# Taking the mean squares of attention results by pairs of tiles beside the last head

## The chip, the core and the metric

The kernel runs on one core of one Trainium2 chip. The metric is the device time of one execution in microseconds (us). Three runs of the kernel before took 2566.53 to 2570.46 us; their median is 2568.71 us.

## The reference, cut to what matters

One post-norm layer is computed for 2048 prompt frames and 8 streams of 16 new frames, 2176 tokens in all. A combined projection feeds a gated convolution and a differential attention of 4 heads with 128 values each. The attention result of each token and head is divided by its root mean square before the output projection:

```python
def rms_norm(x, g):
    xf = x.astype(jnp.float32)
    ms = jnp.square(xf).mean(-1, keepdims=True)
    return (xf * lax.rsqrt(ms + LN_EPS) * g.astype(jnp.float32)).astype(x.dtype)
...
    attn_o = rms_norm(attn_o, subln_g) * (1.0 - lambda_init)
    mixed = jnp.concatenate([y_conv, attn_o.reshape(B, S, ATTN_DIM)], axis=-1)
    x1 = layer_norm(ALPHA * x + jnp.einsum('bse,ed->bsd', mixed, w_out), ln1_g, ln1_b)
```

The mean runs over the 128 values of one head. After this come a feed-forward part (1024 to 4096 to 1024, squared ReLU) and a second layer norm.

## The kernel before, in words

The tokens are 17 tiles of 128 (NT = 17; tile 16 holds the new frames). Everything on TensorE (PE) is fp32 or made of split high and low parts (`mm3`, lines 71 to 73: three matmuls per product). The program has three stages.

1. The input projection (to about 500 us in the trace) writes q, k, v and the gated convolution result to DRAM.
2. The attention loop (lines 874 to 894) walks over head h = 0 to 3 and, in each head, over pairs of query tiles jp = 7 down to 0 (tiles 2jp and 2jp+1). Each pair has a front (scores, maxima, exponentials) and a back (scaling, transposes, values). `merge` interleaves by cost the front of one pair with the back of the pair before and with a share of the fill. The fill is 17 x 9 steps that multiply the convolution result by its half of w_out (`conv_half`, L841 to L867) and write the sum with the residual to `mixd` in DRAM. `finish_av` (L561 to L564) copies the result of one pair out of PSUM (tile `af`) and writes it to `attn` in DRAM with SP's queue. The tile of new frames is done inside each head beside jp = 6, 5, 4 (`decode_steps`).
3. The output projection of the attention half, then the feed-forward part. For each tile t in `ORDER` (11, 16, 10, 15, 9, 14, 8, 13, 7, 12, 6, 5, 4, 3, 2, 1, 0) three helpers are called:
   - `mix_rms(t)` (L933 to L946) loads the tile's four heads from `attn` (L936, SP's queue, tile `at`), squares them on ScalarE (ACT, L938, tile `sq`), takes the means over the partitions with four one-column matmuls against a column of 1/128 (`meand`, L941; each fp32 matmul is two instructions), copies the 128 x 4 result (L943, VectorE, DVE) and forms the inverse root in `rstd_of` (L896 to L909: a square root on ACT, L899, and a Newton step of five small DVE instructions).
   - `mix_prep(t, at, rms)` (L948 to L963) loads the sum so far from `mixd` (L953, tile `z`), builds four diagonal matrices from the roots (L957, tile `dg`), spreads them with matmuls (L958), multiplies `at` by them (L960) and splits the product (cast to high part on ACT, L64, low part on DVE, L67).
   - `mix_out(t, z, m)` (L981 to L994) makes the 24 matmuls of the projection, adds `z` and, for five tiles, a layer norm; `turn` (L494) transposes those five for the feed-forward part.

Three tiles go through `mix_rms` and two through `mix_prep` in the last `merge` (L966), beside the back of the last pair; then `mix_rms` runs three tiles ahead of `mix_out` and `mix_prep` two.

The tile framework orders the instructions of each engine with a timeline of its own: among instructions that are ready it takes the one that stands first in the program. So loads and weight preparation (L134 to L137, L536) are found earlier in the trace than in the program. Each engine then runs its list in order. Buffers matter as well: tiles with the tag `z` of the pool `mp` have three buffers, which the convolution part, `w_out` loads and two of three tiles of `mix_prep` share; `at` and `sq` share four; the PSUM banks `pt` are three.

## Time and profile before

| what | us |
|---|---|
| runs, lowest, median, highest | 2566.53, 2568.71, 2570.46 |
| the profiled execution's own time | 2571.69 |
| its span, first to last instruction | 2569.9 |
| TensorE (PE) busy | 2469.0 |
| VectorE (DVE) busy | 1877.1 |
| ScalarE (ACT) busy | 1291.4 |
| GpSimd (POOL) busy | 914.0 |
| mean granted PE clock | 0.986 of 2.4 GHz |

How to read it: the span is one execution taken by the profiler; the time of an execution is about 1.8 us longer than its span. Busy time is the union of an engine's instructions. Instructions overlap on PE, and their ends are modelled, so that two matmuls with starts 0.23 us apart have durations of 0.39 us each. "[0.97 <-DVE ml L67]" behind an instruction means that its engine stood 0.97 us before it, and that the instruction on line 67 that writes tile `ml` on DVE ended the wait. Times in a timeline count from the span's start.

### The profile page before, as it was taken

To read this page: it belongs to the slowest core of one execution; us is meant where nothing else is said; L and a number is where in the kernel's file an instruction comes from. 1 tells how busy PE (TensorE), PEld (TensorE's weight loads), DVE (VectorE), ACT (ScalarE), POOL (GpSimd) and SP (SyncE) were. 2 spreads that over 40 slices of the span, in tenths; PEclk is the share of its full clock that TensorE was granted. 3 is DMA by queue.
4 is the path that set the end of the run, shared out by engine and by line. 5 is a ranking of instruction groups with operands and counts; after the bars stand their busy time and mean duration, and the time that the engine had idled before them with its cause. 6 is when DMAs were issued, how large, how long until landed. Compare 5 with 4: busy or idle time off the path is not lost. (4 is left out here: it accounts for less than half of the span.)

```text
span 2569.9 us, 38835 instructions
## 1 busy us (share of the span) xinstructions
PE 2469.0 (96%) x13420; PEld 2243.4 (87%) x13420; DVE 1877.1 (73%) x3103; ACT 1291.4 (50%) x2676; POOL 914.0 (36%) x778
## 2 busy tenths in 40 slices
PE   8999999979999999999998999999998999999998
PEld 7999999968787878779997999999997888888886
DVE  7798677767767776786887888898877535444578
ACT  5444445436757666434677566756553322223231
POOL 5565564547465645231232322322223102115000
PEclk9999999999999999999998999999999999999999
DMA  7437326345535343545678577766667655446444
GB/s 250 156 106 233 127 84 191 104 128 181 166 103 157 118 130 107 193 160 172 197 255 291 190 243 244 274 212 209 216 222 267 213 163 185 148 143 221 153 151 148
DMA packets 273317, 463.24 MB, mean 180 GB/s; under 512 B 32320, under 2 KB 178832, under 8 KB 273120
## 3 DMA queue, kind: packets, MB, share of 16 engines
q1 hardware_dynamic: 260160, 431.58, 51.9%
q10 hardware_dynamic: 11088, 24.12, 2.4%
q0 software_dynamic: 1872, 5.07, 0.6%
q8 instruction: 105, 1.72, 0.3%
q14 instruction: 92, 0.75, 0.1%
HBM read 316.98 MB, written 143.69 MB: 179 GB/s over the span
## 5 line engine op out<-in xcount | busy, mean ns | idle before, releaser
L71 PE MATMUL y<-vh,hrh 128*128 128x512 f32 x832 | 323.1, 393 | 5.6 <-ACT vh L64 5.6
L72 PE MATMUL y<-vl,hrh 128*128 128x512 f32 x832 | 323.9, 389 | 1.5 <-DVE vl L67 1.5
L73 PE MATMUL y<-vh,hrl 128*128 128x512 f32 x832 | 323.5, 389 | 0.0
L64 ACT CAST hrh<-hraw 128x1024 fp32r<-128x1024 f32 x112 | 118.1, 1056 | 344.7 <-PE y L72 328.8
L67 DVE TENSOR_TENSOR hrl<-hraw,hrh 128x1024 fp32r<-128x1024 f32 x112 | 146.0, 1304 | 171.6 <-ACT hrh L64 171.3
L686 ACT ACTIVATE p<-s,nm 128x512 f32<-128x512 f32 (+3 forms) x320 | 199.2, 633 | 98.3 <-DVE nm L684 88.5
L684 DVE TENSOR_REDUCE nm<-s 128x1 f32<-128x512 f32 (+3 forms) x320 | 184.5, 601 | 43.9 <-PE s L679 41.9
L71 PEld LDWEIGHTS y<-vh,hrh 128*128 128x128 f32 x832 | 157.8, 190 | 39.4 <-ACT vh L64 6.5
L72 PEld LDWEIGHTS y<-vl,hrh 128*128 128x128 f32 x832 | 156.3, 188 | 34.6 <-DVE vl L67 2.0
L73 PEld LDWEIGHTS y<-vh,hrl 128*128 128x128 f32 x832 | 156.3, 188 | 32.4
L713 POOL TENSOR_SCALAR p<-p,cf 128x512 f32<-128x512 f32 (+3 forms) x160 | 123.9, 793 | 149.7 <-DVE cf L706 124.0
L134 POOL TENSOR_TENSOR wS<-raw 128x512 f32<-128x512 f32 x78 | 113.6, 1457 | 166.2 <-DVE wS1l L67 100.4
L678 PE MATMUL s<-kt,aq 128*128 128x512 f32 (+3 forms) x344 | 136.5, 405 | 18.5 <-DMA kt<-k_sc 10.7
L762 PE MATMUL pa<-a,vt 128*128 128x256 f32 (+1 forms) x576 | 140.3, 371 | 0.4 <-ACT a L741 0.4
L71 PE MATMUL pf<-x11h,w11h 128*128 128x384 f32 (+1 forms) x324 | 108.7, 336 | 15.9 <-ACT x11h L64 14.5
L679 PE MATMUL s<-kt,ql 128*128 128x512 f32 (+3 forms) x344 | 123.2, 366 | 0.3 <-DMA ql<-q_sc 0.3
L762 PEld LDWEIGHTS pa<-a,vt 128*128 128x128 f32 x576 | 104.2, 191 | 14.5 <-ACT a L741 1.2
L1233 POOL TENSOR_TENSOR t<-wq,t 128x512 f32<-128x512 f32 x32 | 51.9, 1636 | 173.1 <-DMA wq<-w_ff 172.8
L71 PE MATMUL pf<-x22h,wS4h 128*128 128x384 f32 (+1 forms) x324 | 107.2, 331 | 3.9 <-DVE c L182 3.8
L72 PE MATMUL pf<-x11l,w11h 128*128 128x384 f32 (+1 forms) x324 | 108.4, 335 | 1.1 <-DVE x11l L67 1.1
L71 PE MATMUL pf<-x21h,w12h 128*128 128x384 f32 (+1 forms) x324 | 105.8, 327 | 3.2 <-ACT u L174 3.2
L73 PE MATMUL pf<-x11h,w11l 128*128 128x384 f32 (+1 forms) x324 | 107.8, 333 | 0.0
(644 smaller groups left out, 7830.2 us busy)
## 6 DMA issues: line engine op xcount, KB each, us to landing
raw<-w_ff SPq DMA_DIRECT2D x96, 512.0 KB, 4.0
hraw<-hf SPq DMA_DIRECT2D x96, 512.0 KB, 4.1
wq<-w_ff SPq DMA_DIRECT2D x144, 256.0 KB, 3.8
raw<-w_in SPq DMA_DIRECT2D x70, 512.0 KB, 4.3
hf<-h SPq DMA_DIRECT2D x32, 768.0 KB, 3.8
wr<-w_ff SPq DMA_DIRECT2D x32, 512.0 KB, 4.3
xs<-x1d SPq DMA_DIRECT2D x24, 512.0 KB, 5.6
hf<-h SPq DMA_DIRECT2D x32, 384.0 KB, 3.2
```

Of the source, the lines that this page charges most:

```text
L64: nc.scalar.copy(hi, src)
L67: return lo_eng.tensor_sub(lo, src, hi)
L71: nc.tensor.matmul(ps, lh, rh, start=start, stop=False, skip_group_check=more)
L72: nc.tensor.matmul(ps, lh, rl, start=False, stop=False, skip_group_check=more)
L73: nc.tensor.matmul(ps, ll, rh, start=False, stop=stop, skip_group_check=more)
L134: nc.gpsimd.tensor_add(S["S1"], a21, a22)
L678: nc.tensor.matmul(ss[c][:, pos:pos + m], aq[:, c, qsl], kt[:, c], start=True, stop=False)
L679: nc.tensor.matmul(ss[c][:, pos:pos + m], ql[:, c, qsl], kt[:, c], start=False, stop=True)
L684: nc.vector.tensor_reduce(nm[:, qb, ci, c:c + 1], s[:, :kn], axis=AX.X, op=ALU.max, negate=True)
L686: nc.scalar.activation(pt[:, :kn], s[:, :kn], AF.Exp, bias=nm[:, qb, ci, c:c + 1], accum_out=sm[:, qb, ci, c:c + 1])
L713: nc.gpsimd.tensor_scalar(p1[:, :kn], p1[:, :kn], X["cf"][:, qb, ci, 1:2], 1.0, op0=ALU.mult, op1=ALU.mult)
L762: nc.tensor.matmul(o, vt[:, kb % 4, :], a[:, i], start=first, stop=end)
```

## The change

The squares of all tiles are taken for pairs of tiles. For tiles 2 to 16 these steps (`squares`) are put into the back of the next pairs of the last head (h = 3), a quarter of the way in: each loads two tiles of `attn` at once, squares them with one ACT instruction, makes the one-column matmuls of both and copies the means into a table `msq`. Both tiles of a step, the loaded one and the squared one, are `z` buffers of the pool `mp`. Tiles 2 and 3 are taken in the back of the last pair; tile 16 by itself in the back of pair 3. The inverse roots of tiles 2 to 16 are then formed by one call of `rstd_of` on 128 x 60 in the middle of that last back, followed by `mix_prep` of the first two tiles of `ORDER`. Tiles 0 and 1 are squared behind the last `merge`, and their roots are a second call. `mix_rms(t)` per tile is gone; `mix_prep(t)` loads `at` itself, so that each tile of `attn` is read twice. The scratch tiles of `rstd_of` are slices of one tile of the probability pool.

```diff
+        msq = mp_.tile([P, NT, H], F32, name="msq", bufs=1)
+        rms = mp_.tile([P, NT, H], F32, name="rms", bufs=1)
+
+        def squares(t, n):
+
+            def put():
+                at = mp_.tile([P, 4, 2 * P], F32, name="z", bufs=3)[:, :, :n * P]
+                nc.sync.dma_start(at, attn[:, :, t * P:(t + n) * P].rearrange("h p t -> p h t"))
+                sq = mp_.tile([P, 4, 2 * P], F32, name="z", bufs=3)[:, :, :n * P]
+                nc.scalar.activation(sq, at, AF.Square)
+                ps = ps_t.tile([P, 512], F32, name="pt")
+                for i in range(n):
+                    for h in range(H):
+                        k = i * H + h
+                        nc.tensor.matmul(ps[:, k:k + 1], sq[:, h, i * P:(i + 1) * P], meand, start=True, stop=True)
+                nc.vector.tensor_copy(msq[:, t:t + n].rearrange("p n h -> p (n h)"), ps[:, :n * H])
+            return put
...
             pend = back
+            if h == H - 1 and jp < 7:
+                pend.insert(len(pend) // 4, (0.3, squares(2 * jp + 2, 2)))
+            if h == H - 1 and jp == 3:
+                pend.insert(len(pend) // 2, (0.2, squares(NT - 1, 1)))
...
-        def mix_rms(t):
-            s = slice(t * P, (t + 1) * P)
+        class Slices:
+
+
+            def __init__(self, pool):
+                self.home, self.used = pool.tile([P, 512], F32, name="rm", tag="p"), 0
+
+            def tile(self, shape, dtype, name):
+                self.used += shape[1]
+                return self.home[:, self.used - shape[1]:self.used]
+
+        def mix_rms(a, n):
+
+            flat = lambda x: x[:, a:a + n].rearrange("p n h -> p (n h)")
+            rstd_of(Slices(pp), flat(rms), flat(msq), [P, n * H], "rm")
+
+        def mix_prep(t):
             at = mp_.tile([P, 4, P], F32, name="at", bufs=4)
-            nc.sync.dma_start(at, attn[:, :, s].rearrange("h p t -> p h t"))
-            sq = mp_.tile([P, 4, P], F32, name="sq", tag="at", bufs=4)
-            nc.scalar.activation(sq, at, AF.Square)
-            mp = ps_t.tile([P, 512], F32, name="pt")
-            for h in range(H):
-                nc.tensor.matmul(mp[:, h:h + 1], sq[:, h, :], meand, start=True, stop=True)
-            ms = mp_.tile([P, H], F32, name="ms")
-            nc.vector.tensor_copy(ms, mp[:, :H])
-            rms = mp_.tile([P, H], F32, name="rms")
-            rstd_of(mp_, rms, ms, [P, H], "rm")
-            return t, at, rms
-
-        def mix_prep(t, at, rms):
+            nc.sync.dma_start(at, attn[:, :, t * P:(t + 1) * P].rearrange("h p t -> p h t"))
...
-                nc.vector.tensor_scalar(dg, ident, rms[:, h:h + 1], None, op0=ALU.mult)
+                nc.vector.tensor_scalar(dg, ident, rms[:, t, h:h + 1], None, op0=ALU.mult)
...
-        q_rms, q_prep = [], []
-        merge(pend, fill, [(0.2, lambda t=t: q_rms.append(mix_rms(t))) for t in ORDER[:AHEAD + 1]]
-              + [(0.9, lambda: q_prep.append(mix_prep(*q_rms.pop(0))))] * AHEAD)
+        q_prep = []
+        def mix_first(t):
+            return 0.9, lambda: q_prep.append(mix_prep(t))
+
+        mid = len(pend) // 2
+        pend[mid:mid] = [(0.2, lambda: mix_rms(2, NT - 2))] + [mix_first(t) for t in ORDER[:AHEAD]]
+        merge(pend, fill)
+        squares(0, 2)()
+        mix_rms(0, 2)
...
-            if i + AHEAD + 1 < NT:
-                q_rms.append(mix_rms(ORDER[i + AHEAD + 1]))
-            if q_rms:
-                q_prep.append(mix_prep(*q_rms.pop(0)))
+            if i + AHEAD < NT:
+                q_prep.append(mix_prep(ORDER[i + AHEAD]))
```

## Rows read from the trace of the kernel before

**Rows 1.** The page, first section: engine, busy us, share of the span, instructions.

```profile
PE 2469.0 (96%) x13420; PEld 2243.4 (87%) x13420; DVE 1877.1 (73%) x3103; ACT 1291.4 (50%) x2676; POOL 914.0 (36%) x778
```

**Rows 2.** Windows: stretch; busy PE, PEld, DVE, ACT, POOL (instructions); PE clock, DMA share, GB/s.

```profile
1000.00:1053.00 53.00, 49.32 (x286) 41.87 (x285) 37.65 (x115) 31.29 (x87) 26.15 (x34) 1.00 0.48 148
1053.00:1198.00 145.00, 136.57 (x719) 116.79 (x719) 114.37 (x318) 47.36 (x90) 30.18 (x20) 0.95 0.47 163
1075.00:1090.00 15.00, 13.03 (x61) 11.00 (x61) 11.68 (x44) 4.77 (x10) 2.40 (x1) 0.77 0.41 140
1110.00:1125.00 15.00, 12.82 (x75) 10.81 (x76) 13.48 (x38) 4.03 (x9) 5.31 (x4) 1.00 0.60 211
1145.00:1160.00 15.00, 13.11 (x64) 11.18 (x63) 11.56 (x35) 5.28 (x12) 4.34 (x3) 0.77 0.69 227
```

**Rows 3.** Timeline of PE, 1060 to 1150 us: start, us, instruction, [idle before <-releaser].

```profile
1067.65 0.50 PE L73 MATMUL s<-woh,ml 128*128 128x512 f32 x1 [0.97 <-DVE ml L67]
...
1077.03 0.79 PE L71 MATMUL s<-woh,mh 128*128 128x512 f32 x1 [1.97 <-ACT mh L64]
...
1110.46 1.13 PE L958 MATMUL pt<-dg,onesd 128*128 128x128 f32 x8 [1.65 <-DVE x22l L67]
...
1115.70 0.71 PE L958 MATMUL pt<-dg,onesd 128*128 128x128 f32 x4 [1.29 <-DVE dg L957]
...
1147.15 1.18 PE L941 MATMUL pt<-cols,sq 128*128 128x1 f32 x6 [1.89 <-ACT sq L938]
```

**Rows 4.** Tile sq: its matmuls; durations in ns, minimum, median, maximum.

```profile
L941 PE MATMUL pt<-cols,sq x136: 164/250/353, 1041.2 to 1171.6; 128*128 128x1 f32 x136
```

**Rows 5.** Timeline of PE from the last pairs' values to the first projection matmul.

```profile
1041.19 1.84 PE L941 MATMUL pt<-cols,sq 128*128 128x1 f32 x16
...
1044.83 1.68 PE L762 MATMUL pa<-a,vt 128*128 128x256 f32 x8
...
1047.03 0.40 PE L73 MATMUL pt<-wch,ml 128*128 128x512 f32 x1
1048.78 1.05 PE L941 MATMUL pt<-cols,sq 128*128 128x1 f32 x8 [1.35 <-ACT sq L938]
...
1050.05 1.06 PE L958 MATMUL pt<-dg,onesd 128*128 128x128 f32 x8
...
1052.74 0.50 PE L71 MATMUL s<-woh,mh 128*128 128x512 f32 x1
```

**Rows 6.** Timeline of ACT, 1040 to 1050 us.

```profile
1041.83 1.28 ACT L899 ACT_TABLE_LOAD   x1
...
1048.09 0.63 ACT L938 ACTIVATE sq<-at 128x512 f32<-128x512 f32 x1 [4.48 <-DMA at<-attn]
1048.63 0.35 ACT L563 COPY af<-pa 128x256 f32<-128x256 f32 x1
```

**Rows 7.** Tile rms: diagonals and one of the small steps; ns, minimum, median, maximum.

```profile
L957 DVE TENSOR_SCALAR dg<-ident,rms x68: 255/281/746, 1044.3 to 1174.9; 128x128 f32<-128x128 f32 x68
L900 DVE RECIPROCAL rms<-rmsd x17: 158/172/179, 1043.5 to 1172.7; 128x4 f32<-128x4 f32 x17
```

**Rows 8.** Timeline of DVE ahead of PE's stop at 1077.03 us.

```profile
1075.52 0.15 DVE L943 COPY ms<-pt 128x4 f32<-128x4 f32 x1
1075.59 0.74 DVE L960 SCALAR_TENSOR_TENSOR at<-at,cols,pt 128x512 f32<-128x512 f32 x1
```

**Rows 9.** Source line L564, 860 to 1060 us: writes of attention results, 17 of them.

```profile
DMA to landing us min/median/max: 1.7/2.5/5.3
```

**Rows 10.** Source line L936: loads of one tile of attention results (256 KB), 17 of them.

```profile
DMA to landing us min/median/max: 2.8/3.7/11.1
```

**Rows 11.** Source line L826: loads of 512 KB of w_out, four of them.

```profile
DMA to landing us min/median/max: 4.3/4.4/4.5
```

**Rows 12.** Source line L1094: Squares of 1024 columns on ACT, in ns.

```profile
L1094 ACT ACTIVATE sq<-xs,mean x12: 1139/1152/1157, 1198.2 to 1583.4; 128x1024 f32<-128x1024 f32 x12
```

**Rows 13.** Lines, ACT, 1000 to 1200 us: the casts; busy us, mean ns, idle before, releasers.

```profile
L64 ACT CAST mh<-at 128x512 fp32r<-128x512 f32 x17 | 10.5, 619 | 22.4 <-DVE at L960 14.3 <-PE s L72 5.8 <-DVE dg L957 2.3
```

## The prediction

> **What bounds the kernel now.** I read the page's first section before anything else: the matrix engine PE is busy 96% of the span [rows 1], so only two kinds of change can move the end: one in the work that PE does, or one in the time that PE stands or runs slowly. The table of windows then shows the two stretches that the change touches. From 1000 to 1053 us, the end of the last head's attention, PE works 49.32 of 53 us at full clock. From 1053 to 1198 us, which is the output projection and the first products after it, PE works 136.57 of 145 us, so it stands 8.4 us, and its clock is below one: 0.77 in each of two stretches of 15 us [rows 2]. The clock has two levels, 2.4 and 1.2 GHz, so a mean of 0.77 loses 0.23 x 15 = 3.45 us, 6.9 us for both. VectorE (DVE) works 114.37 of the same 145 us, far more than ScalarE (ACT): it is the busiest helper there [rows 2]. PE's timeline names the stops: five of them, of 0.97, 1.97, 1.65, 1.29 and 1.89 us, make 7.8 of the 8.4 us, and what ended them is DVE or ACT work each time [rows 3]. The two low clocks stand behind the stops of 1.97 and 1.89 us; behind 1.65 and 1.29 us the clock stayed at 1.00 [rows 2, 3].
>
> **PE's work is moved, not removed.** The mean squares are 136 one-column matmuls before [rows 4] and stay 136. Sixteen of them in a row take 1.84 us [rows 5], so 17 tiles hold 17 x 8 x 0.115 = 15.6 us. Three tiles' worth stands before 1053 us already [rows 5]; fifteen will (tiles 2 to 16). So about 12 tiles, 11 us, move forward from one stretch where PE is the limit to another: by itself zero. What they can fill in the last head is its idle time, 53 - 49.32 = 3.7 us [rows 2], less the stop of 1.35 us [rows 5] that lies at the change-over below: 2.3 us, of which I take 1.5 (bounds 0 and 2.3).
>
> **New waits in the last head.** Each pair loads its results again by SP's queue, squares them on ACT and needs a "z" buffer for each of the two. ACT serves in order, and a Square put ahead of its data holds what stands behind it: before, one held ACT 4.48 us and a finished result (af) stood behind it [rows 6], and one of the three groups of mean squares in this stretch stopped PE, by 1.35 us [rows 5]. Eight groups move into stretches with exponentials on ACT. At one stop in three this is 8 x 1.35 / 3 = 3.6 us; with other attention work beside them it is zero. I take 0.5, near zero, because ACT's 4.48 us of waiting became only 1.35 us of PE. The second reading of the results adds 17 x 0.26 = 4.5 MB to 148 GB/s x 53 us = 7.8 MB at a DMA share of 0.48 [rows 2]; that is hidden while the queues are half empty, and its price, if not, is a longer landing, in the bounds of the change-over. The three buffers are shared with the loads of x for the convolution part, which run late by a pair's stay; those are needed four matmul groups later, so I price them at nothing; without that cover they would add to the 3.6 us. Together: -1.0 us (bounds -2.3 and +3.6).
>
> **The projection stretch gets freer.** Each tile loses a load wait, a Square of 0.63 us [rows 6], a square root and six small DVE instructions, of which the reciprocal of four columns takes 0.17 us [rows 7]; 15 tiles x 6 x 0.17 = 15 us of DVE's 114, replaced by two rounds. The stop of 1.89 us waited for a Square itself: it goes, with the clock behind it, 5.3 us. The stop of 1.97 us was PE waiting for a cast whose input (at, L960) stood in DVE's queue behind a copy of another tile's mean squares (L943) and what came before it [rows 3, 8]: with a shorter queue it probably goes, with its clock, 5.4 us. The stops of 0.97 and 1.29 us are DVE's backlog too; I count half, 1.1 us. The 1.65 us waits for buffers of the transposes and stays. Against that, tiles 0 and 1 are now squared inside this stretch, late, since their second buffer comes free only when an earlier tile's z does: one more stop like the 1.35 us at two chances in three, 0.9 us. Sum -11 us; the bounds are -5.3 (only the stop that names the Square) and -14.7 (all five and the clock).
>
> **The change-over gets a chain.** This is what the change pays with. Before, the first projected tile (11) has its own roots, from data written long before, and PE starts the projection at 1052.74 us, 6.2 us after the values of the last pair but one end (1044.83 + 1.68 = 1046.5) [rows 5]. After, every tile needs the batch of tiles 2 to 16, and tiles 2 and 3 are that same pair. From the end of its values: copy 0.35, write landing 2.5, load of 512 KB 4.4 (as long as the weights of that size; 3.7 is the median of today's half-size load) [rows 6, 9, 10, 11], Square of 1024 columns 1.15 [rows 12], 16 matmuls 1.84 [rows 5], copy, root and five small steps 7 x 0.18 = 1.3 [rows 7], four diagonals 4 x 0.28 = 1.1 [rows 7], the last of the broadcasts 0.3 of 1.06 [rows 5], the product with "at" 0.74 [rows 8], the cast 0.62 [rows 13]; about eleven hand-overs of 0.06 us (a Square's end at 1048.72 to its matmul at 1048.78 [rows 5, 6]) add 0.7. That makes 15 us. PE's work in it: the 4.9 us it had in those 6.2 us, with 1.84 in place of 0.92 for the squares, 5.8 us, and half of the pair before, 0.9. It stands 8.4 us where it stood 1.35: +7.0. A stop of that length I expect to be followed by the low clock, as the shorter ones of 1.97 and 1.89 us were: +3.4. Sum +10.4 us. Bounds: with the shortest landings (1.7 and 2.8) [rows 9, 10], the whole pair before as filling and no low clock, +3.7; with the longest (5.3 and 11.1) it would be about +20. I take the medians: the queues are half empty (a DMA share of 0.48 [rows 2]), and 11.1 is one landing of 17.
>
> The rows price write and load at 2.5 and 4.4 us [rows 9, 11], and I put one after the other. The Trainium skill, "DMA: Bandwidth & Descriptors", section "Two DMAs through the same engine are not ordered", speaks against the change here: a load of what another DMA writes has to wait for that one's completion, even on the same queue. No row here shows an overlap; with one, the sum would be 2.5 us lower. The same page of the Trainium skill ("Anatomy of one DMA") gives some 2 us as the fixed part of a DMA and 436 GB/s for the rest; an estimate from it is 2.3 and 3.2 us, 1.4 us less than the rows, and the sum would be 1.4 us lower by it. The rows decide.
>
> The square root's table load (1.28 us, once [rows 6]) stays one, since no exponential follows the first root: zero, and in the standing time anyway.
>
> **Sum.** -1.0 - 11 + 10.4 = -1.6 us. The profiled execution took 2571.69 us (span 2569.9), 2.98 us over the median of the runs shown, 2568.71. Against its own time the sum is 2570.1; against the median 2567.1, my forecast: 2567.0. A measurement of this kernel can tell about 0.2% from no change, 5.1 us, so that this is "same". The likeliest case's own range is 2563 to 2574.
>
> **Rivals.**
> A, faster: the change-over is covered. If landings are short and PE has the earlier pairs' squares and convolution left over for it, it costs +3.7 while the projection gives 13 to 14.7: -10 to -12 us, 2557 to 2559. For it: DVE is busy 79% of the projection stretch [rows 2], and weight preparation would move into the standing time. Against: the last convolution matmul ends at 1047.43 us, 0.9 us behind the point where that chain begins [rows 5], so that little is left to cover it.
> B, slower: the chain decides. The place is the batch of roots, which waits for the last loaded pair; the price is +14 (a landing of some 6 us more, or ACT's 4.48 us wait placed ahead of af, then the low clock), with -6 from the projection and +1 in the head: +9, 2578. It decides from the point at which that chain passes some 18 us. For it: landings up to 11.1 us [rows 10]. Against: no wait of that kind stopped PE by more than 1.97 us before [rows 3, 5]. The Trainium skill, "TensorE: Matmul & The Clock Gate", Part 1, says that idleness brings the half clock back; the trace agrees behind two of six stops.
> C, the moved Squares do not leave the projection: buffers hold the pairs back until attention ends, and all that is left of the change is fewer small instructions. Then -3 to +3 us, inside the forecast's range.
>
> **How the numbers follow.** Forecast with C 0.37, A 0.34, B 0.29. Gains and loss are of one size and each is uncertain by half of itself, so no case dominates; A is a little ahead of B, since the two stops with the low clock both hang on work that leaves, and the landings must be worse than median for B. The range is 2556 to 2579: it takes in A's -12 and B's +9, and leaves about one in five outside, on the slow side mostly. Faster 0.34, same 0.37, slower 0.29.
>
> **What will show it.** Right: PE's stops that wait for a Square or for "at" gone from the projection, clock 1.00 there but for its beginning; one stop of some 8 us, or two of 4, between the last attention values and the first projection matmul; the batch's root on ACT standing at its end; DVE below 100 us in the projection. Wrong: a change-over without a stop of over 4 us (A), one of over 11 us or a stop at squares inside the head (B), or a changed order of the attention itself, which I price at nothing.

## The result: 81 us slower, and nearly all of it before the projection

The changed kernel takes 2649.03 us (median of four runs, 2648.28 to 2656.83) and the kernel before 2567.82 us beside it: a ratio of 1.0316, 95% interval 1.0303 to 1.0329. The forecast was 2567.0 us, "same", with a range of 2556 to 2579. The profiled execution took 2648.28 us (span 2646.2).

### The profile after

First section of the page of the changed kernel (engine, busy us, share of the span, instructions), which answers to [rows 1]:

```profile
PE 2505.3 (95%) x13420; PEld 2273.7 (86%) x13420; DVE 1872.7 (71%) x3020; ACT 1284.3 (49%) x2653; POOL 916.7 (35%) x778
```

PE has as many instructions as before and is busy 36 us longer with them; the span of the profiled execution is 76 us longer, so that PE also stands 40 us more. Four points of PE's timeline say where:

| point, us from the span's start | before | after |
|---|---|---|
| first value matmul of the last head (pa, L762) | 947.4 | 945.6 |
| first matmul of the output projection | 1052.7 | 1134.1 |
| end of its last matmul | 1192.5 | 1272.9 |
| end of the span | 2569.9 | 2646.2 |

So the last head takes 189 us where it took 105, the projection 139 where it took 140, and the rest is 4 us shorter. These are windows of the changed kernel (columns as in [rows 2]): the last head, the projection, and three pieces of the last head:

```profile
945.00:1134.00 189.00, 139.94 (x651) 120.80 (x651) 72.44 (x181) 69.75 (x172) 58.65 (x69) 0.76 0.31 91
1134.00:1273.00 139.00, 125.94 (x589) 104.43 (x588) 104.64 (x233) 34.84 (x61) 29.52 (x19) 0.93 0.49 166
...
1060.00:1080.00 20.00, 11.73 (x55) 10.97 (x55) 0.33 (x2) 3.83 (x6) 0.00 (x0) 0.58 0.32 106
1080.00:1100.00 20.00, 11.75 (x53) 10.12 (x51) 2.07 (x3) 3.45 (x6) 0.00 (x0) 0.74 0.15 46
1100.00:1120.00 20.00, 8.36 (x31) 7.23 (x31) 0.18 (x2) 2.49 (x4) 0.00 (x0) 0.61 0.30 89
```

In the last head PE stands 189 - 139.94 = 49.1 us; before it stood 105 - 96.86 = 8.1 us. Its busy time grew from 96.9 to 139.9 us: 11 us are the mean squares that moved here (the forecast's 12 tiles), and some 32 us are the clock, 0.98 before and 0.76 now. In the last three rows nothing else works either: DVE 0.2 to 2 us of 20, POOL nothing, a DMA share of 0.15 to 0.32. That is a chain of latencies and no engine that is full.

PE's timeline names the wait. All nine groups of mean squares (L883), with the values of two pairs, the transposes behind the first group and a convolution matmul:

```profile
967.36 1.68 PE L762 MATMUL pa<-a,vt 128*128 128x256 f32 x8
...
976.22 3.57 PE L883 MATMUL pt<-cols,z 128*128 128x1 f32 x16 [6.26 <-ACT z L878]
979.66 1.09 PE L737 MATMUL pt<-ident,p 128*128 128x128 f32 x4
...
1008.89 3.55 PE L883 MATMUL pt<-cols,z 128*128 128x1 f32 x16
...
1042.06 3.51 PE L883 MATMUL pt<-cols,z 128*128 128x1 f32 x16
...
1068.27 3.58 PE L883 MATMUL pt<-cols,z 128*128 128x1 f32 x16 [10.98 <-ACT z L878]
...
1072.59 1.71 PE L883 MATMUL pt<-cols,z 128*128 128x1 f32 x8
...
1077.61 2.54 PE L762 MATMUL pa<-a,vt 128*128 128x256 f32 x12
...
1087.15 3.58 PE L883 MATMUL pt<-cols,z 128*128 128x1 f32 x16 [7.00 <-ACT z L878]
...
1106.34 3.57 PE L883 MATMUL pt<-cols,z 128*128 128x1 f32 x16 [7.59 <-ACT z L878]
...
1122.07 3.58 PE L883 MATMUL pt<-cols,z 128*128 128x1 f32 x16 [7.29 <-ACT z L878]
...
1126.08 0.63 PE L72 MATMUL pt<-wcl,mh 128*128 128x512 f32 x1
...
1150.37 3.58 PE L883 MATMUL pt<-cols,z 128*128 128x1 f32 x16 [4.48 <-ACT z L878]
```

Six of the nine stop PE, five of them in the last head (39.1 of its 49.1 us), the sixth in the projection. Sixteen of these instructions take 3.5 us where they took 1.84 [rows 5]. The table of waits of the changed kernel says the same in two lines (engine, tile and line, what it waited for, us, times, longest):

```profile
PE pt L883 <- ACT z L878: 43.6, 6, 11.0
...
ACT z L878 <- DMA z<-attn: 31.5, 5, 8.5
```

Follow one stop, the 7.00 us that end at 1087.15, through the timelines of ACT and of SP (the changed kernel):

```profile
1080.19 0.37 ACT L563 COPY af<-pa 128x256 f32<-128x256 f32 x1 [1.74 <-PE pa L762]
...
1086.04 1.06 ACT L878 ACTIVATE z<-z 128x1024 f32<-128x1024 f32 x1 [5.48 <-DMA z<-attn]
...
1149.07 0.29 ACT L921 ACTIVATE l1sd<-l1mv,cols 128x1 f32<-128x1 f32 x1 [13.77 <-DVE l1mv L939]
1149.28 1.04 ACT L878 ACTIVATE z<-z 128x1024 f32<-128x1024 f32 x1
```

```profile
1080.59 0.33 SPq L564 DMA_DIRECT2D attn<-af  x1
1082.34 0.37 SPq L876 DMA_DIRECT2D z<-attn  x1
...
1134.82 0.38 SPq L564 DMA_DIRECT2D attn<-af  x1
...
1138.83 0.38 SPq L876 DMA_DIRECT2D z<-attn  x1
```

The pair's last values end at 1077.61 + 2.54 = 1080.15. Copy to `af` at 1080.19, write issued at 1080.59, the load of the same data issued 1.75 us later, Square 3.70 us after that, 1.06 us of Square, matmuls at 1087.15. Copy, write, load, Square: 7.0 us from PE to PE through DRAM, with nothing in PE's list between the values of a pair and its mean squares. The Trainium skill, "DMA: Bandwidth & Descriptors", section "Two DMAs through the same engine are not ordered", says that a load of what another DMA writes must wait for that one's completion. By that rule the trace agrees: the load leaves 1.75 us after the write here, and the nine writes of this stretch took 1.5, 1.7 and 5.3 us to land (minimum, median, maximum). The other two lines of each view are the sixth stop, tiles 0 and 1: that load left 4.0 us after the write, with other loads between, and its Square stood on ACT behind a layer norm's root that waited 13.77 us for DVE. So this stop is one of ACT's order and not of the trip alone.

### The profile page after: what moved, and what is told of

Its sections match the earlier page's. It is cut to its first block, busy times and chain, and to the rows that moved or that the text cites. A ratio compares the mean times of both kernels' runs of the same rounds, so it can differ in the third digit from the quotient of the medians.

```text
span 2646.2 us, 38741 instructions
## 1 busy us (share of the span) xinstructions
PE 2505.3 (95%) x13420; PEld 2273.7 (86%) x13420; DVE 1872.7 (71%) x3020; ACT 1284.3 (49%) x2653; POOL 916.7 (35%) x778
## 4 chain that ended last, share of the span: by engine, by line
PE 80%; DVE 6%; DMA 6%; issue 3%; ACT 2%; POOL 2%; SPq 1%; ACTq 0%; DVEq 0%; POOLq 0%
PE pf L71 13%; PE pf L73 13%; PE pf L72 13%; PE y L71 8%; PE y L72 8%; PE y L73 8%; PE pa L762 3%; PE pt L737 2%; PE s L678 2%; PE s L679 1%; PE pt L71 1%; PE s L71 1%; PE s L72 1%; PE s L73 1%; PE pt L72 1%
## 5 line engine op out<-in xcount | busy, mean ns | idle before, releaser
L762 PE MATMUL pa<-a,vt 128*128 128x256 f32 (+1 forms) x576 | 142.8, 376 | 0.1
L741 ACT COPY a<-pt 128x512 f32<-128x512 f32 x144 | 78.6, 569 | 83.3 <-PE pt L737 77.8
L762 PEld LDWEIGHTS pa<-a,vt 128*128 128x128 f32 x576 | 106.0, 194 | 14.6 <-ACT a L741 1.2
L678 PEld LDWEIGHTS s<-kt,aq 128*128 128x128 f32 x344 | 67.3, 197 | 49.6 <-ACT p L686 34.1
```

Source lines behind the costliest of these rows:

```text
L678: nc.tensor.matmul(ss[c][:, pos:pos + m], aq[:, c, qsl], kt[:, c], start=True, stop=False)
L762: nc.tensor.matmul(o, vt[:, kb % 4, :], a[:, i], start=first, stop=end)
```

## Experiments

In the tables below "head" runs from the first value matmul of the last head to the first projection matmul, and "projection" from there to the end of its last matmul, both by PE's timeline; "stands" is the length less PE's busy time in the windows view, and the clock is of the same window. Ratios are to runs of the kernel before on the same chip, with 95% intervals; the level of the kernel before differs by up to 4 us from chip to chip, so differences between two kernels are taken from their ratios, times 2570 us.

| kernel | median us | ratio | head, stands, clock | projection, stands |
|---|---|---|---|---|
| before | 2567.82 | 1 | 105, 8.1, 0.98 | 140, 8.4 |
| after | 2649.03 | 1.0316 [1.0303, 1.0329] | 189, 49.1, 0.76 | 139, 13.1 |
| own_z | 2644.19 | 1.0281 [1.0260, 1.0301] | 187, 50.7, 0.79 | 135, 13.1 |
| tile_roots | 2658.90 | 1.0338 [1.0317, 1.0359] | 188, 49.7, 0.76 | 146, 19.5 |
| own_bank | 2635.35 | 1.0253 [1.0236, 1.0270] | 147, 21.7, 0.84 | 139, 14.6 |
| free_src | 2586.21 | 1.0055 [1.0035, 1.0076] | 122, 7.7, 0.92 | 142, 14.5 |

### Which part of the changed step makes PE stand

The theory on trial was the trip through DRAM; its rivals were the shared buffers, the batch of roots and the shared PSUM bank. Four kernels, each the changed kernel with one edit.

**own_z**: the loaded and squared tiles get two buffers of their own instead of `z`.

```diff
+        sqp = pa.enter_context(pool("sqp", 2))
...
-                at = mp_.tile([P, 4, 2 * P], F32, name="z", bufs=3)[:, :, :n * P]
+                at = sqp.tile([P, 4, 2 * P], F32, name="sqz")[:, :, :n * P]
...
-                sq = mp_.tile([P, 4, 2 * P], F32, name="z", bufs=3)[:, :, :n * P]
+                sq = sqp.tile([P, 4, 2 * P], F32, name="sqz")[:, :, :n * P]
```

> The changed kernel, but loaded and squared tiles get two buffers of their own in place of the three z buffers shared with the convolution part. Theory 'buffers': the stops ahead of the one-column matmuls shrink to a few us and the time falls below 2600 us. Theory 'bank': the order on the matrix engine is that of the changed kernel and the loads still wait for the writes: 2630 to 2660 us, stops of 4 to 11 us as before.

PE's timeline of own_z, two of its groups:

```profile
1089.24 3.57 PE L884 MATMUL pt<-cols,sqz 128*128 128x1 f32 x16 [7.04 <-ACT sqz L879]
...
1147.40 1.84 PE L884 MATMUL pt<-cols,sqz 128*128 128x1 f32 x16
```

The stops in the head stay; only the one for tiles 0 and 1, in the projection, goes. The buffers are worth 5 us by the medians and 9 by the ratios (1.0316 less 1.0281; two runs), and the trace has 4 of them in the projection.

**tile_roots**: tiles 2 to 16 get their roots one by one in `mix_prep`.

```diff
         def mix_prep(t):
+            if t > 1:
+                rstd_of(mp_, rms[:, t], msq[:, t], [P, H], "rm")
...
-        pend[mid:mid] = [(0.2, lambda: mix_rms(2, NT - 2))] + [mix_first(t) for t in ORDER[:AHEAD]]
+        pend[mid:mid] = [mix_first(t) for t in ORDER[:AHEAD]]
```

> The changed kernel with its moved squares, but the roots of tiles 2 to 16 are formed tile by tile ahead of the first use, as in the kernel before, so that the first projected tile needs no batch. Theory 'roots' (my prediction's change-over chain): the chain of some 15 us before the projection goes and with it 10 to 20 us. Theory 'bank': the stops inside the head stay and the planner still puts the last pair's squares ahead of the projection: 2640 to 2655 us.

The head does not change (188 us), and the projection gets 7 us longer. The time, 2658.90 us, lies 4 us above the range of theory 'bank' and far from theory 'roots'. The batch costs nothing; if anything it gives a little.

**own_bank**: the means get a PSUM bank of their own, taken from the four of the scores.

```diff
-        ps_s = ph.enter_context(pool("ps_s", 4, space=PSUM))
+        ps_s = ph.enter_context(pool("ps_s", 3, space=PSUM))
+        ps_q = ph.enter_context(pool("ps_q", 1, space=PSUM))
...
-                ps = ps_t.tile([P, 512], F32, name="pt")
+                ps = ps_q.tile([P, 512], F32, name="pq")
```

> The changed kernel, but the means of the pairs get a PSUM bank of their own, taken from the four score banks (three are left), instead of one of the three banks that the attention's transposes use. Theory 'bank': the transposes' banks are handed out in program order, so the transposes of the next pair stand behind the squares of the last one, which wait 7 to 11 us for write, load and Square; then most of the 81 us go: 2560 to 2590 us, no stop over 4 us ahead of a group of one-column matmuls before the last pair. Theory 'buffers' (the loads are late for lack of z buffers) and theory 'roots' (the batch of roots): nothing much changes, over 2630 us.

PE's timeline of own_bank: its stops over 1 us ahead of mean squares, and, ahead of the first of them, the pair's last values and the next pair's transposes:

```profile
1018.48 1.97 PE L763 MATMUL pa<-a,vt 128*128 128x256 f32 x8
...
1022.94 1.03 PE L738 MATMUL pt<-ident,p 128*128 128x128 f32 x8
1025.05 1.95 PE L884 MATMUL pq<-cols,z 128*128 128x1 f32 x16 [1.08 <-ACT z L879]
...
1048.66 3.58 PE L884 MATMUL pq<-cols,z 128*128 128x1 f32 x16 [2.65 <-ACT z L879]
...
1104.38 3.57 PE L884 MATMUL pq<-cols,z 128*128 128x1 f32 x16 [7.76 <-ACT z L879]
1109.44 3.58 PE L884 MATMUL pq<-cols,z 128*128 128x1 f32 x16 [1.48 <-ACT z L879]
```

That is only 16 us by the ratios, far short of the 2560 to 2590 us that theory 'bank' named, but the head shrinks from 189 to 147 us: the two do not fit until one asks what the lost score bank costs. **before_s3** and **after_s3** are the two kernels with three score banks and nothing else changed (`pool("ps_s", 3, ...)`).

> Kernel before with three PSUM banks for scores and not four: the control for own_bank, which took its bank from there. If the bank lost costs nothing: within 5 us of the kernel before, and the 14 us that own_bank gained are all that a bank of its own gives. If the score banks matter: 15 us or more slower than the kernel before, and a bank of its own would give that much more than own_bank showed.

> The changed kernel with three score banks and not four: the control for own_bank, which has the same three and one bank for the mean squares alone. If the bank of the transposes, shared with mean squares that wait, is a part of the loss: about 2675 to 2685 us (the 30 us of three score banks on top of 2649), so that a bank of its own gives 40 to 50 us; its stops ahead of the one-column matmuls stay at 6 us and more. If a bank of its own gives only the 14 us seen: about 2650.

before_s3 took 2601.46 us, 1.0115 [1.0100, 1.0130]; after_s3 2669.13 us, 1.0378 [1.0360, 1.0396], a little below its expected range. Three score banks cost the kernel before some 30 us (the changed kernel 16), most of them ahead of the last head: its first value matmul stands at 973.9 us (before_s3), 971.6 (after_s3) and 973.0 (own_bank) against 947.4. So a bank of its own gives 1.0378 less 1.0253, some 32 us, and the head says so too (183 to 147 us). With a shared bank the group of means stands in one row with the transposes of the next pair, which then follow it in PE's list; with its own, transposes and scores go ahead of it and cover most of the trip. One long stop is left, of 7.76 us at the last pairs, where nothing is left to go ahead.

**free_src**: the load reads another tensor, written in the first stage, so that it does not wait for a write; the means are then those of other data.

```diff
-                nc.sync.dma_start(at, attn[:, :, t * P:(t + n) * P].rearrange("h p t -> p h t"))
+                nc.sync.dma_start(at, yc[:, :, t * P:(t + n) * P].rearrange("h p t -> p h t"))
```

> The changed kernel, but the pairs are loaded from the convolution result (same shape and size, written long before) and not from the attention result, so the means are of other data; banks, buffers, number of loads and matmuls stay. It takes away the wait of the load for the write alone. Theory 'bank' in its second half (the squares wait on the round trip through DRAM): below 2600 us, the stops ahead of one-column matmuls mostly gone. Theory 'buffers': over 2630 us.

PE's timeline of free_src, its last groups:

```profile
1052.46 1.84 PE L883 MATMUL pt<-cols,z 128*128 128x1 f32 x16
...
1056.53 1.84 PE L883 MATMUL pt<-cols,z 128*128 128x1 f32 x16
...
1082.31 3.46 PE L883 MATMUL pt<-cols,z 128*128 128x1 f32 x16 [4.68 <-ACT z L878]
```

No group stops PE in the head any more, and PE stands 7.7 us there, as before the change (8.1), at the same bank, buffers, Squares and bytes. 1.0316 less 1.0055 is 67 us: so much of the 81 us is the wait for the pair's own write and load, with the low clock that comes with it. One stop is left, of 4.68 us for tiles 0 and 1 in the projection. Of the 17 us by which the head is still longer, 11 are the matmuls moved here.

### Can the trip be covered, or left out?

| kernel | median us | ratio | head, stands, clock | projection, stands |
|---|---|---|---|---|
| later | 2601.04 | 1.0111 [1.0096, 1.0126] | 129, 15.6, 0.91 | 145, 16.4 |
| direct | 2582.68 | 1.0041 [1.0026, 1.0056] | 108, 7.3, 0.97 | 130, 9.4 |
| direct_4 | 2583.33 | 1.0042 [1.0028, 1.0056] | 105, 7.8, 0.98 | 136, 12.6 |
| hybrid | 2575.93 | 1.0020 [1.0010, 1.0029] | 120, 11.4, 0.96 | 129, 8.7 |
| hybrid_late | 2574.21 | 1.0010 [1.0000, 1.0020] | 120, 9.9, 0.94 | 127, 6.9 |
| hybrid_dg7 | 2575.44 | 1.0016 [1.0005, 1.0027] | 122, 8.8, 0.91 | 132, 7.0 |
| hybrid_early | 2574.39 | 1.0015 [1.0004, 1.0026] | 116, 6.1, 0.96 | 123, 6.4 |
| before_dg7 | 2567.99 | 0.9989 [0.9980, 0.9999] | 105, 8.2, 0.98 | 137, 6.7 |

**later**: the changed kernel with each pair's means put in one pair later.

```diff
-            if h == H - 1 and jp < 7:
-                pend.insert(len(pend) // 4, (0.3, squares(2 * jp + 2, 2)))
+            if h == H - 1 and jp < 6:
+                pend.insert(len(pend) // 4, (0.3, squares(2 * jp + 4, 2)))
...
-        pend[mid:mid] = [(0.2, lambda: mix_rms(2, NT - 2))] + [mix_first(t) for t in ORDER[:AHEAD]]
+        pend[mid:mid] = [(0.2, lambda: mix_rms(4, NT - 4))] + [mix_first(t) for t in ORDER[:AHEAD]]
...
+        squares(2, 2)()
         squares(0, 2)()
-        mix_rms(0, 2)
+        mix_rms(0, 4)
```

> Changed kernel with each pair's mean squares put in one pair later (the pair of tiles 2 and 3 and tiles 0 and 1 behind the attention, roots in batches of 13 and 4 tiles). All operations are the same. Theory round trip (PE stands because result, write to DRAM, load and Square, some 8 to 10 us in a row, are shorter than nothing that stands between in PE's order): with a whole pair's work of 13 to 20 us between, the stops ahead of the one-column matmuls inside the head fall below 2 us each, the clock there goes back above 0.9, and the time comes to 2570 to 2590 us, about what free_src gave; one stop for tiles 2, 3, 0, 1 may be left at the end. Rival order (the one-column matmuls and their PSUM bank displace the next pair's transposes, whenever their data come): the stops stay at 5 us and more wherever the groups stand, and the time stays at 2630 to 2655.

PE's timeline of later, the last four groups:

```profile
1050.87 1.95 PE L883 MATMUL pt<-cols,z 128*128 128x1 f32 x16 [0.50 <-ACT z L878]
...
1062.37 3.58 PE L883 MATMUL pt<-cols,z 128*128 128x1 f32 x16 [6.16 <-ACT z L878]
...
1089.93 3.58 PE L883 MATMUL pt<-cols,z 128*128 128x1 f32 x16 [4.81 <-ACT z L878]
...
1094.97 3.57 PE L883 MATMUL pt<-cols,z 128*128 128x1 f32 x16 [1.46 <-ACT z L878]
```

The same operations, one place later, give 53 us back. The early groups are covered; the short pairs at the end of a head are not, with stops of 6.16 and 4.81 us where less than 2 us was expected inside the head, and the median misses its range (2570 to 2590) by 11 us.

**direct**: ScalarE squares the finished result in SBUF in every head, and the second load is gone. **direct_4** has the roots in batches of 13 and 4 tiles.

```diff
             nc.sync.dma_start(attn[h, :, t0:t0 + n], af[:, :n])
+            sqf = stp.tile([P, 256], F32, name="sqf")
+            nc.scalar.activation(sqf[:, :n], af[:, :n], AF.Square)
+            ps = ps_t.tile([P, 512], F32, name="pt")
+            for i in range(n // P):
+                nc.tensor.matmul(ps[:, i:i + 1], sqf[:, i * P:(i + 1) * P], meand, start=True, stop=True)
+            nc.vector.tensor_copy(msq[:, t0 // P:(t0 + n) // P, h], ps[:, :n // P])
...
-                pend.insert(len(pend) // 4, (0.3, squares(2 * jp + 2, 2)))
...
-        squares(0, 2)()
```

> Mean squares taken beside the result itself: in every head ScalarE squares the finished 128x256 result in SBUF and PE reduces it by two one-column matmuls; the second load and the 17 group loads are gone, roots in batches of 15 and 2 tiles. The count of one-column matmuls stays 136. Theory round trip: no DRAM is left in the chain, only copy, Square (about 0.5 us) and hand-overs, about 1 us; 34 groups may stop PE by 0 to 0.7 us each, the clock stays near 0.98: 2560 to 2590 us, below free_src if the 34 groups are mostly covered. Rival order: 34 groups in PE's order right behind the values, each displacing transposes, cost as the six did in the changed kernel: over 2640.

> As direct, but with roots in batches of 13 and 4 tiles, so that the first projected tiles do not wait for the pair of tiles 2 and 3. Theory of the prediction (the chain at the change-over is a cost of its own): 3 to 8 us faster than direct, and the stop ahead of the first broadcasts shrinks. Rival (that chain is short once no DRAM lies in it): within 3 us of direct.

PE's timeline of direct, three of its groups:

```profile
1056.83 0.61 PE L569 MATMUL pt<-cols,sqf 128*128 128x1 f32 x4 [0.97 <-ACT sqf L566]
...
1064.77 0.61 PE L569 MATMUL pt<-cols,sqf 128*128 128x1 f32 x4 [0.91 <-ACT sqf L566]
...
1070.75 0.61 PE L569 MATMUL pt<-cols,sqf 128*128 128x1 f32 x4 [0.91 <-ACT sqf L566]
```

Without DRAM the chain is 0.9 us. The head is then 108 us and the projection 130, 8 us less than before the change in sum. It is paid for earlier: the last head begins at 970.9 us against 947.4, for the same groups now stand in the heads before as well, and the matmuls of three heads that moved there are some 12 of these us (17 tiles x 3 heads x 2 instructions of 0.115 us). The other order of the roots changes nothing in the median, where the prediction's theory had 3 to 8 us. In direct_4 the last head begins at 964.4 us, though nothing ahead of it was edited: 6 us between two single traces can be chance.

**hybrid** joins the two: heads 0 to 2 are loaded most of a pair ahead (they were written long before), and head 3 is squared from SBUF. **hybrid_late** puts the matmuls one pair later, with roots in batches of 13 and 4.

```diff
+            if h == H - 1 and n == 2 * P:
+                SQ[t0] = sqp.tile([P, 2 * P], F32, name="sqf")
+                nc.scalar.activation(SQ[t0], af, AF.Square)
...
+                EARLY[t] = sqp.tile([P, 3, 2 * P], F32, name="sqe")
+                nc.sync.dma_start(EARLY[t], attn[:3, :, t * P:(t + 2) * P].rearrange("h p t -> p h t"))
+                nc.scalar.activation(EARLY[t], EARLY[t], AF.Square)
...
-                pend.insert(len(pend) // 4, (0.3, squares(2 * jp + 2, 2)))
+                pend.insert(len(pend) // 4, (0.3, sqpair(2 * jp + 2)))
+            if h == H - 1:
+                pend.insert(len(pend) // 2, (0.0, sqload(2 * jp)))
```

> Heads 0 to 2 of a pair are loaded and squared most of a pair ahead (their results are long since written), head 3 of the last head is squared from SBUF as its result is copied; the eight one-column matmuls stand where the changed kernel has them. The same operations on PE; no data of a group passes through DRAM late. Theory round trip: no stop ahead of a one-column matmul over 1.5 us; from the first value matmul of the last head to the first projection matmul 110 to 120 us (before 105, after 189, the kernel that loads old data 122, with 11 us of matmuls moved here), the projection 128 to 142 us; in all 2560 to 2585 us. Rival (a shared bank and order cost even when the data are there): that stretch stays over 135 us and the time over 2600.

> As hybrid, but the one-column matmuls stand one pair later and the roots are taken in batches of 13 and 4 tiles, so that even the copy and Square of about 1 us are covered. Theory round trip: within 6 us of hybrid (there is little left to cover), 2558 to 2582 us. Rival (each group in PE's order costs by its place): 10 us or more away from hybrid.

Both came as the theory had it, 76 and 79 us below the changed kernel, with no wait for data of the same pair: 1.0020 and 1.0010 times the kernel before. (One group in hybrid stops PE by 1.62 us, over the 1.5 expected; it waits for a copy of transposes, L746, and not for a Square.) PE's timeline of hybrid_late, its three largest stops from the last head's middle to the projection's end:

```profile
1060.78 2.47 PE L1007 MATMUL pt<-dg,onesd 128*128 128x128 f32 x10 [3.63 <-DVE dg L1006]
...
1118.63 2.02 PE L1007 MATMUL pt<-dg,onesd 128*128 128x128 f32 x8 [2.31 <-DVE at L1009]
...
1151.73 0.94 PE L1007 MATMUL pt<-dg,onesd 128*128 128x128 f32 x6 [3.50 <-DVE at L1009]
```

None waits for a Square. Three kernels asked about them. **hybrid_dg7** is hybrid_late with seven buffers for the diagonals and not four (`name="dg", bufs=7`) and two, not three, for the early squares; **before_dg7** has the seven in the kernel before; and **hybrid_early** forms the roots of tiles 6 to 16 at the beginning of the last pair's back:

```diff
+        pend[0:0] = [(0.2, lambda: mix_rms(6, NT - 6))]
         mid = len(pend) // 2
-        pend[mid:mid] = [(0.2, lambda: mix_rms(4, NT - 4))] + [mix_first(t) for t in ORDER[:AHEAD]]
+        pend[mid:mid] = [mix_first(t) for t in ORDER[:AHEAD]]
...
-        mix_rms(0, 4)
+        mix_rms(0, 6)
```

> hybrid_late with seven buffers for the diagonals and not four (and two, not three, for the early squares). Open from the prediction: the projection was to get 11 us shorter beyond the matmuls that leave it, and hybrid_late still shows three stops of 2.3 to 3.6 us ahead of broadcasts there. If the four diagonal buffers hold the broadcasts of the second of two tiles back: those stops fall below 1.5 us each, with the clock behind them, and the time falls by 6 to 14 us to 2560 to 2568, below the kernel before. If it is VectorE's own queue that is late: the stops stay, within 4 us of hybrid_late (2574).

> The kernel before with seven buffers for the diagonals: the control for hybrid_dg7. Its stops ahead of broadcasts are 1.65 us (buffers of the transposes) and 1.29 us (a diagonal): if the diagonals' buffers matter it gains 2 to 5 us; if VectorE's queue is late, it stays within 2 us of the kernel before.

> hybrid_late with the first batch of roots 11 tiles large (6 to 16), at the beginning of the last pair's back, so that the square root's table load (1.28 us), the root and the first diagonals no longer stand behind the last mean squares. In hybrid_late 3.63 us of PE standing at the change-over lie in that chain (means at 1057.18, first broadcasts at 1060.78 us). If the prediction's term for the change-over is real and is what remains: that stop falls below 1 us, and the time falls by 3 to 7 us, to 2567 to 2571, at or just below the kernel before. If another wait takes its place (VectorE's queue): within 2 us of hybrid_late (2574).

PE's timeline of hybrid_dg7:

```profile
1128.16 2.08 PE L1007 MATMUL pt<-dg,onesd 128*128 128x128 f32 x8 [3.38 <-DVE at L1009]
...
1161.74 2.08 PE L1007 MATMUL pt<-dg,onesd 128*128 128x128 f32 x8 [2.85 <-DVE at L1009]
```

The stops stay with seven buffers, so the diagonals' buffers are not what holds them. They end with VectorE's product (L1009), which reads the PSUM bank of the broadcasts: VectorE is late with it, and what it frees is a bank. How many banks the broadcasts have was not varied. In hybrid_early the stop of 3.63 us is gone, and from the last head's first values to the projection's end it takes 239 us, where the kernel before takes 245. The median did not follow (2574.39 against hybrid_late's 2574.21): in the profiled execution the 6 us are back to 1.6 by the end of the span. Runs of hybrid_early lie between 2568 and 2579 us, so that a gain of 3 us cannot be told from none; where it goes stays open. No version beats the kernel before by more than 0.2%. before_dg7 comes nearest, 0.11% below it [0.0001 to 0.0020 below]. That is 2.8 us, inside the 2 to 5 us that its expectation gave to the buffers, and the stop of 1.29 us at a diagonal is gone from its trace; but the interval reaches down to 0.3 us, too little to build on.

## Why the prediction was wrong

**The step that failed** is "New waits in the last head", priced at +0.5 us with a bound of +3.6. Measured, the wait for the pair's own data carries 67 us (free_src), with its clock. The step took its price from the one row that looked alike, a stop of 1.35 us at one group in three [rows 5]. But the groups in that row squared tiles 11, 16 and 10, which had been written whole pairs before; what they waited for was a load. The change squares a pair a quarter of a pair after its values, and the wait is copy, write, load and Square in a row. The prediction had that chain, at 0.35 + 2.5 + 4.4 + 1.15 = 8.4 us without hand-overs, and it was a fair price: the stop traced above has 0.37 + 1.75 + 3.70 + 1.06, with hand-overs 7.0 us. It was charged once, at the change-over, where the text says that every tile needs the last pair. It was due at every pair. Five of eight pairs paid it in full or nearly, and the clock took about three quarters as much again (32 us beside 41).

**What made it due** is the list of PE, which the prediction priced at nothing ("a changed order of the attention itself"). Before, the next pair's transposes ran ahead of the last values of a pair. After, the group of means stands right behind the pair's values, and the transposes behind the group (967.36, 976.22 and 979.66 us in the timeline above). PE's timeline of the kernel before, at the same pair, the next pair's transposes and the pair's last values:

```profile
966.55 0.66 PE L737 MATMUL pt<-ident,p 128*128 128x128 f32 x4 [1.11 <-ACT st L583]
...
971.83 0.81 PE L762 MATMUL pa<-a,vt 128*128 128x256 f32 x4
```

The bank of its own shows it: with three score banks, 32 us of the loss hang on that order. They lie at least in part within the 67 us, since the two together exceed the 81. In free_src, with the shared bank, no group stops PE in the head: data that are there can stand in that place.

**The change-over** was forecast at 8.4 us of standing PE and the low clock. The stop for tiles 2 and 3 is 7.29 us, with convolution matmuls of 0.63 us behind it where one took 0.40 at full speed [rows 5]. The mechanism was right and the size near: from the end of the pair's values (1114.79) to the first projection matmul (1134.13) it takes 19.3 us where it took 6.2, so 13.1 us more for the 10.4 forecast, at a granted clock of 0.65. The square root's table load was rightly free there: on ACT it begins at 1122.03 us and runs beside the mean squares on PE, and the root then still waits 2.57 us for the means. In hybrid_late, where it comes after the means (its msq stands at 1057.18 us), it is 1.28 of the 3.63 us. Rows of ACT's timeline, first of the changed kernel, then of hybrid_late:

```profile
1122.03 1.28 ACT L921 ACT_TABLE_LOAD   x1
1125.88 0.34 ACT L921 ACTIVATE rm<-msq,cols 128x60 f32<-128x60 f32 x1 [2.57 <-DVE msq L884]
```

```profile
1057.42 1.28 ACT L946 ACT_TABLE_LOAD   x1 [0.44 <-DVE msq L892]
```

**The projection** was to get 11 us shorter beside the 11 us of matmuls that leave it. It is 139 us for 140: less the matmuls, 10 us longer where 11 us shorter was forecast. A part is the sixth stop, for tiles 0 and 1: 4.48 us and the low clock behind it, where the prediction had 0.9. In the versions without late data the gain beside the matmuls is 2 us (hybrid_late, 127 us) or 5 (hybrid_early, 123 us). The stop that named a Square and the one that named a cast are gone; in their place PE stands ahead of broadcasts, in the changed kernel for 2.76 and 3.07 us, until VectorE has done a product or a diagonal. VectorE's busy time fell from 112.2 to 104.6 us, not below 100. The small steps of the roots that left took 23.5 us there (the table of lines, 14 tiles), more than the 15 counted. But the diagonals went from 14.1 us (58 of them) to 22.5 (57). In hybrid_late the six single diagonals that take over 0.7 us (0.76 to 1.54, where the median is 0.28) all run beside a GpSimd instruction and end 0.08 or 0.09 us behind its end. Rows of hybrid_late ahead of the stop of 3.50 us, of VectorE's timeline and then of GpSimd's:

```profile
1148.05 1.54 DVE L1006 TENSOR_SCALAR dg<-ident,rms 128x128 f32<-128x128 f32 x1
...
1150.93 0.74 DVE L1009 SCALAR_TENSOR_TENSOR at<-at,cols,pt 128x512 f32<-128x512 f32 x1
```

```profile
1147.15 2.35 POOL L978 TENSOR_TENSOR z<-z,gb 128x1024 f32<-128x1024 f32 x1 [7.37 <-DVE z L977]
```

So work was taken out of VectorE's queue, and a part came back as waiting beside GpSimd. No run moved GpSimd's work: this is read off the traces, and what it costs in time is not shown.

**Right by size**: the moved matmuls are zero by themselves (hybrid_late: head +15, projection -13); the three shared buffers (own_z, 5 to 9 us), the batch of roots (tile_roots) and the second reading (a DMA share of 0.31 in the head) are small. Rival B had the sign and, in what would show it, "a stop at squares inside the head"; its 2578 us allowed for one such chain.

**What is left**: free_src is 14 us above the kernel before. Its head is 17 us longer, 11 of them the moved matmuls, and its projection did not get shorter for losing them (142 us). What holds VectorE back there was tried only by the diagonals' buffers: neither GpSimd's work beside it nor the number of PSUM banks was varied.

## What to carry to other kernels

When a consumer is moved towards its producer, write down how old its data are at the new place, and charge the whole chain from producer to consumer at every place where it is younger than that chain; a wait measured on old data says nothing about fresh data. On an in-order engine it is the place in the list that costs, and a shared PSUM bank or buffer fixes that place without a word in the code. If the data must be fresh, take them from SBUF: 0.9 us here, against 7 through DRAM.

## What the runs showed of the hardware that was not expected

- **The clock adds to the stops.** In the last head 41 us more standing came with some 32 us of slower matmuls. Behind each of the long stops the mean squares and what follows run at half rate (3.58 us for sixteen against 1.84; 0.63 us apiece for convolution matmuls), and the granted clock of whole stretches of 20 us was 0.58 to 0.74, where 0.5 is the lower of its two levels, 1.2 GHz. The Trainium skill, "TensorE: Matmul & The Clock Gate", Part 1, says that idleness brings this on. By that rule the trace agrees, six stops of six; of the six stops that the prediction names in the kernel before it was two. Not all of the 32 us lie behind long stops: the groups at 1008.89 and 1042.06 us ran at half rate too, and the stops in the 6 us ahead of each were at most 1.22 and 2.25 us. From 1000 to 1057 us the granted clock was 0.79, where in the kernel before it was 1.00.
- **A PSUM bank less for the scores cost some 30 us** (before_s3): by the profiled execution 27 of 34 us lie ahead of the last head: 16 us in stops of at most 2.8 us (the one of 10.5 us at the beginning of the attention the kernel before has too, 10.7), the rest in PE's busy time.
- **A load behind a write of the same data** was issued 1.7 to 5.4 us after that write in the last head (1080.59 to 1082.34; 1057.81 to 1063.21), and the load's own landing was 3.7, 3.9 and 9.8 us (minimum, median, maximum of nine): the wait for the write is a quarter of the trip of 7.0 us and half of the one of 10.98. The 5.4 us are not the shared buffers: with buffers of its own (own_z) the same load left 5.1 us after its write.
- **A small VectorE instruction can last as long as the GpSimd instruction beside it**: diagonals of 0.28 us took up to 1.54 us in hybrid_late and ended 0.08 or 0.09 us behind GpSimd's end.
